# RMS norms of the differential heads in the grouped part, map combination split over two engines, grouped values in pairs

## The chip, the core and the metric

The kernel runs on one core of one Trainium2 chip. Its metric is the device time of one execution in microseconds (us), from launch to end, as the median of several runs. A core has five engines that each take their instructions in a fixed order and wait for one another by semaphores: TensorE (PE; its weight loads are shown apart as PEld), VectorE (DVE), ScalarE (ACT), GpSimd (POOL) and SyncE (SP, which issues the DMAs). Matmul results go to PSUM; the rest lies in SBUF.

## What is computed

A trunk of two layers over 1024 latent tokens with 256 context tokens in front, width 1024. The first layer's mixer is attention with two kinds of heads in parallel; the second layer's is a gated convolution; each layer has an MLP. The change lies in the first layer's attention, cut here to what matters:

```
def diff_attention(q, k, v, lam, lam_init, subln_g):      # 4 heads, each with two maps of width 64
    s = jnp.einsum('bqhid,bkhid->bhiqk', q, k) * (HEAD_DIM ** -0.5)
    p = jax.nn.softmax(s.astype(jnp.float32), axis=-1)
    attn = (p[:, :, 0] - lam * p[:, :, 1]).astype(v.dtype)
    o = jnp.einsum('bhqk,bkhe->bqhe', attn, v)
    o = rms_norm(o, subln_g) * (1.0 - lam_init)

def gqa_attention(q, k, v):                               # 8 query heads on 2 key/value heads
    s = jnp.einsum('bqgrd,bkgd->bgrqk', q, k) * (HEAD_DIM ** -0.5)
    p = jax.nn.softmax(s.astype(jnp.float32), axis=-1).astype(v.dtype)
    o = jnp.einsum('bgrqk,bkgd->bqgrd', p, v)
```

Queries are the 1024 latent tokens, keys all 1280 tokens.

## The kernel before

Attention is two stages, one after the other: the differential heads (some 291 to 516 us in the trace), then the grouped heads (to some 775 us). A scheduler orders each engine's instructions from the order in which the code emits them, with `high_priority` moving some forward; a tile's buffers are a ring of `bufs`, and an instruction that writes a tile waits until the buffer's last user is done.

**Differential stage.** `Attention.build` walks 32 steps: 4 heads, 4 units of 256 queries in each head, 2 steps of 128 queries in a unit. One step (`UnitA.scores`) makes two maps of 128 queries by 1280 keys. For each, `softmax` has TensorE write the scores `s` into three PSUM banks (L1135 and L1136; the ring of `s` holds two maps), VectorE find the row maxima `mx` (L1138), and ScalarE take the exponential `e` with its row sum `sm` (L1141). VectorE then combines the maps in one instruction over all 1280 keys, `e0 += cc * e1` (L1254), with `cc` from the two row sums (L1251, L1252). Two steps later TensorE transposes the combined map in ten pieces of 128 keys (L1150, in three groups of 4, 4 and 2 pieces, each into one PSUM tile `one`, of which there are two), ScalarE copies each group to `pt` (L1155), and per unit TensorE multiplies by the values (L1272), whose result ScalarE copies to `ot` (L1274). The maps aren't divided by their first row sum `s0`, so the RMS norm has a term with the square of `s0`: VectorE squares it (L1259), POOL multiplies the identity by it into `dg` (L1260). After every second unit `finish` does the norm of 512 queries: ACT squares `ot` (L1281), TensorE sums squares and adds the epsilon term (L1283, L1284), ACT copies the result (L1286) and makes a first inverse root in three instructions (L458 to L460), VectorE refines it (L461 to L463) and scales `ot` (L1289). There are eight such norms; six lie wholly between 300 and 510 us.

**Grouped stage.** `Grouped.build` walks 80 steps: eight blocks `j` (a pair of heads and 512 queries), ten key tiles `kt` in each. A step has the score matmuls of its key tile (L1381, L1382), two exponentials on ACT into `pt` (L1383), and the sum of the exponentials over key tiles into `e`, on POOL for `kt` 1 to 6 and on VectorE for 7 to 9 (L1387). For the next block, `maximum` runs ahead: three score matmuls (L1355) and three row maxima on VectorE (L1357) in each of the first eight steps; L1358 joins three maxima into `w`. Five PSUM banks (`bank`) are shared by exponentials and maxima: two and three of them in a step. Two steps later `values` multiplies by the values (L1396): two matmuls of 64 columns each, on the left and right half of TensorE's array. `divide` sums the row sums with ones (L1411, also on array halves), inverts them on ACT (L1414, L1415) and scales the block's result on VectorE (L1416 to L1418).

L1396 and L1411 are the only matmuls on array halves. In what follows a *stretch* is a row of such matmuls with no other matmul between them on TensorE.

Of the kernel before, what the change touches and what calls it, by code (L numbers as in the profile page):

```python
# [9 lines left out]
F32 = mybir.dt.float32  # L10
F32R = mybir.dt.float32r
AF = mybir.ActivationFunctionType
ALU = mybir.AluOpType
# [3 lines left out]
P = 128  # L17
# [7 lines left out]
KT = NC + NT  # L25
KEYS = KT * P
# [4 lines left out]
GROUPS = ((0, 4), (4, 4), (8, 2))  # L31
# [24 lines left out]
class Trunk:  # L56
# [34 lines left out]
    def build(self):  # L91
        nc = self.nc
        nc.scalar.preload_act_table_set("natural_log_exp_and_others")
        with self.pool("const") as cp:
            self.cp = cp
            self.constants()
            with self.pool("one", space=PSUM) as op, self.pool("dram", space=bass.MemoryType.DRAM) as dp:
                self.op, self.dp = op, dp
                self.main()
# [989 lines left out]
class Attention:  # L1089
# [36 lines left out]
                                           in1=q[s][r, :].bitcast(F32), op0=ALU.mult, op1=ALU.subtract)  # L1126
        return q

    def softmax(self, q, c, k):

        nc, pl = self.nc, self.pl
        s = self.pp.tile([P, 1536], F32, name="s", tag="s", bufs=2)
        for (g0, gn), (k1, k2) in zip(GROUPS, k):
            o = s[:, g0 * P:(g0 + gn) * P]
            nc.tensor.matmul(o, lhsT=q[:, c], rhs=k1[:, 0:gn * P], start=True, stop=False)  # L1135
            nc.tensor.matmul(o, lhsT=q[:, c], rhs=k2[:, 0:gn * P], start=False, stop=True)  # L1136
        mx = pl.tile([P, 1], F32, name="mx", bufs=4)
        nc.vector.reduce_max(out=mx, in_=s[:, 0:KEYS], axis=AX.X, negate=True)  # L1138
        e = pl.tile([P, KEYS], F32, name="e", tag="e", bufs=6)
        sm = pl.tile([P, 1], F32, name="sm", bufs=6)  # L1140
        nc.scalar.activation(e, s[:, 0:KEYS], AF.Exp, bias=mx, accum_out=sm)  # L1141
        return e, sm

    def transposed(self, e, pt, i):

        t, nc = self.t, self.nc
        for g, (g0, gn) in enumerate(GROUPS):
# [6 lines left out]
            o, v = pt[g][:, 0:gn, i * P:(i + 1) * P], tr[:, 0:gn * P].rearrange("p (k q) -> p k q", q=P)  # L1154
            nc.scalar.copy(out=o, in_=v)  # L1155

    def build(self):
        t = self.t
        units = self.units
        steps = [(u, i) for u in units for i in range(2)]  # L1160
        n = len(steps)
        psa = t.pool("ps2", space=PSUM)
        self.pp = psa.__enter__()

        def prepare(k):
            if k % 2 == 0 and 2 <= k + 2 < n:
                units[k // 2 + 1].prepare()
            elif k == n - 2:
                self.grouped = Grouped(self)
                self.grouped.prepare(0)  # L1170

        def weights(k):
            if 0 <= k - 2 < n:
                u, i = steps[k - 2]
                u.weights(i)

        def scores(k):
            if k < n:
                u, i = steps[k]
                u.scores(i)  # L1180

        def values(k):
            j = k - 2
            if 0 <= j < n and j % 2 == 1:
                units[j // 2].values()
                if j == n - 1:
                    t.first_weights()

        def finish(k):
            j = k - 4  # L1190
            if 0 <= j < n and j % 4 == 3:
                units[j // 2].finish()

        for k in range(n + 4):
            if k == n:
                psa.__exit__(None, None, None)
                psb = t.pool("ps3", space=PSUM)
                self.grouped.pp = psb.__enter__()
            for f, offset in ((prepare, 200), (weights, 100), (scores, None), (values, 0), (finish, 0)):
                if offset is None:  # L1200
                    f(k)
                else:
                    with t.tc.high_priority(offset=offset):
                        f(k)
            if k >= n:
                self.grouped.first(k - n)
        self.grouped.build()
        psb.__exit__(None, None, None)
# [27 lines left out]
class UnitA(Unit):  # L1236
# [8 lines left out]

    def scores(self, i):
        at, t, nc, pl, c = self.at, self.at.t, self.at.nc, self.at.pl, self.cols(i)
        e0, s0 = at.softmax(self.q[0], c, self.k[0])
        e1, s1 = at.softmax(self.q[1], c, self.k[1])
        cc = pl.tile([P, 1], F32, name="cc", bufs=4)  # L1250
        nc.vector.reciprocal(out=cc, in_=s1)  # L1251
        nc.vector.scalar_tensor_tensor(out=cc, in0=cc, scalar=s0, in1=t.nlam, op0=ALU.mult, op1=ALU.mult)  # L1252

        nc.vector.scalar_tensor_tensor(out=e0, in0=e1, scalar=cc, in1=e0, op0=ALU.mult, op1=ALU.add)  # L1254
        if self.b % 2 == 0 and i == 0:
            UnitA.state["dg"] = pl.tile([P, 512], F32, name="dg", tag="dg", bufs=2)
        self.dg = UnitA.state["dg"]
        c2 = pl.tile([P, 1], F32, name="c2", bufs=4)
        nc.vector.tensor_tensor(out=c2, in0=s0, in1=s0, op=ALU.mult)  # L1259
        nc.gpsimd.tensor_tensor(out=self.dg[:, c], in0=t.ident, in1=c2.broadcast_to([P, P]), op=ALU.mult)  # L1260
        self.e[i] = e0

    def weights(self, i):
# [4 lines left out]
    def values(self):  # L1268
# [3 lines left out]
            nc.tensor.matmul(pv[:, 0:256], lhsT=t.vA[kt][:, h * P:(h + 1) * P], rhs=self.pt[kt // 4][:, kt % 4, :],  # L1272
                             start=kt == 0, stop=kt == KT - 1)
        nc.scalar.copy(out=self.out(), in_=pv[:, 0:256])  # L1274

    def finish(self):

        at, t, nc, pl = self.at, self.at.t, self.at.nc, self.at.pl
        u = self.ot[:, (self.b - 1) * 256:(self.b + 1) * 256]
        sq = t.ut("sq")  # L1280
        nc.scalar.activation(sq, u, AF.Square)  # L1281
        nrm = at.one()
        nc.tensor.matmul(nrm, lhsT=t.sdiv, rhs=sq, start=True, stop=False)  # L1283
        nc.tensor.matmul(nrm, lhsT=t.sepsm, rhs=self.dg, start=False, stop=True)  # L1284
        v = t.ut("v2")
        nc.scalar.copy(out=v, in_=nrm)  # L1286
        y = t.ut("y")
        t.rsqrt0(y, sq, v)
        nc.vector.scalar_tensor_tensor(out=u, in0=u, scalar=t.subg, in1=y, op0=ALU.mult, op1=ALU.mult)  # L1289


class Grouped:

# [78 lines left out]
    def exponentials(self, j, kt):  # L1372
        nc, pl = self.nc, self.at.pl
        k1, k2 = self.k[j // 4][kt // 4]
        c = slice(kt % 4 * P, (kt % 4 + 1) * P)
        pt = self.pt[j, kt] = pl.tile([P, 2, 512], F32, name="pt", tag="pt", bufs=8)
        if kt == 0:
            self.sum[j] = pl.tile([P, KEYS], F32, name="e", tag="e", bufs=6)
        for s in range(2):
            o = self.bank()  # L1380
            nc.tensor.matmul(o, lhsT=k1[:, c], rhs=self.q[j][s], start=True, stop=False)  # L1381
            nc.tensor.matmul(o, lhsT=k2[:, c], rhs=self.q2[j][s], start=False, stop=True)  # L1382
            nc.scalar.activation(pt[:, s, :], o, AF.Exp)  # L1383
        f = self.sum[j][:, 0:1024].rearrange("p (s q) -> p s q", s=2)
        if kt > 0:
            eng = nc.gpsimd if kt < 7 else nc.vector
            eng.tensor_tensor(out=f, in0=self.pt[j, 0] if kt == 1 else f, in1=pt, op=ALU.add)  # L1387
# [40 lines left out]

    def build(self):
        n = 8 * KT  # L1430
        for k in range(n + 5):
            j, kt = divmod(k, KT)
            if k < n:
                if kt == 7 and j + 2 < 8:
                    self.prepare(j + 2)
                self.exponentials(j, kt)
                if j < 7:
                    self.ahead(j + 1, kt)
            if 0 <= k - 2 < n:
                j, kt = divmod(k - 2, KT)  # L1440
                self.values(j, kt)
                if kt == KT - 1:
                    self.finish(j)
            if k >= 5 and (k - 5) % KT == KT - 1:
                self.divide((k - 5) // KT)

    def ahead(self, j, m):
        with self.t.tc.high_priority(offset=40):
# [61 lines left out]
```

## Time and profile before

| | us |
|---|---|
| median of three runs | 2594.61 |
| their range | 2592.67 to 2594.73 |
| profiled execution, whole | 2599.33 |
| profiled execution, span from first to last instruction | 2597.6 |

The profiled execution lies 4.72 us above the median, and 1.7 us of it lie around the span. Over the span PE is busy for 94%, DVE for 75%, ACT for 48%, POOL for 15%. A matmul's busy time in the records includes its way through the array, so that successive matmuls overlap; the distance from one start to the next is the better measure of what a matmul takes from TensorE. The differential stage is about 225 us of the span, the grouped stage about 260 us.

### The profile page before, as it was taken

Reading aid. Unit: us, or ns where it says so; the run is one execution under the profiler, and the core shown is the slowest. Engines: PE = TensorE matmul, PEld = TensorE weight load, DVE = VectorE, ACT = ScalarE, POOL = GpSimd, SP = SyncE. Lnnn points to the kernel's source line nnn. Section 1 sums busy time; section 2 is a strip of 40 time slices with the busy share of each in tenths; the row PEclk is TensorE's granted clock in tenths of the full one; section 3 lists DMA queues with packets and bytes.
Section 4 is the critical chain, followed back from the end, with each engine's and each line's share of the span. In section 5 each row is a group of like instructions: output and inputs, shape, how many; then the busy total and the mean of one; then the engine's idle time right before and its main releaser. Section 6 shows DMA issues by size and latency. Waiting matters only on the chain. (4 is left out here: it accounts for less than half of the span.)

```text
span 2597.6 us, 29924 instructions
## 1 busy us (share of the span) xinstructions
PE 2433.4 (94%) x10706; PEld 1893.6 (73%) x10706; DVE 1946.2 (75%) x2980; ACT 1244.2 (48%) x2018; POOL 392.7 (15%) x245
## 2 busy tenths in 40 slices
PE   5999899999999879999899989999999999899997
PEld 3778677754547667787788777788777888688786
DVE  9877888887868877785756689766888555765867
ACT  3403477755552475454344346533348555334343
POOL 5101000034542410000000023100331000000002
PEclk7999899999999989999899999999999999899999
DMA  5551011000021047777642230123303445844231
GB/s 206 199 180 45 21 30 47 15 25 6 1 65 49 3 141 258 251 254 243 247 138 101 89 122 31 51 73 106 130 25 107 161 138 169 294 145 138 82 122 65
DMA packets 118517, 297.11 MB, mean 114 GB/s; under 512 B 13536, under 2 KB 19296, under 8 KB 118368
## 3 DMA queue, kind: packets, MB, share of 16 engines
q1 hardware_dynamic: 118368, 295.20, 33.8%
q8 instruction: 84, 1.38, 0.2%
q14 instruction: 65, 0.53, 0.1%
HBM read 225.29 MB, written 63.96 MB: 111 GB/s over the span
## 5 line engine op out<-in xcount | busy, mean ns | idle before, releaser
L74 PE MATMUL ps<-bl,part 128*128 128x512 f32 x784 | 308.9, 395 | 7.9 <-DVE bl L78 7.9
L73 PE MATMUL ps<-bh,part 128*128 128x512 f32 x784 | 309.3, 396 | 6.4 <-ACT part L909 6.4
L75 PE MATMUL ps<-bh,part 128*128 128x512 f32 x784 | 308.7, 397 | 5.8 <-DVE part L78 5.8
L909 ACT CAST part<-a 128x512 fp32r<-128x512 f32 x196 | 121.8, 623 | 305.0 <-PE ps L74 161.1
L78 DVE TENSOR_TENSOR part<-a,part 128x512 fp32r<-128x512 f32 x196 | 134.7, 689 | 160.7 <-ACT part L909 160.7
L73 PE MATMUL ps<-T,a 128*128 128x512 f32 x608 | 238.8, 393 | 9.7 <-DVE tmp L818 7.0
L74 PE MATMUL ps<-T,a 128*128 128x512 f32 x608 | 237.9, 391 | 2.2 <-DVE T L78 2.2
L75 PE MATMUL ps<-T,a 128*128 128x512 f32 x608 | 237.8, 391 | 0.0
L529 POOL TENSOR_TENSOR acc<-acc,mb 128x512 f32<-128x512 f32 x29 | 48.1, 1689 | 1074.2 <-ACT mb L526 1074.2
L78 DVE TENSOR_TENSOR a<-raw,a 128x1024 fp32r<-128x1024 f32 (+1 forms) x114 | 119.3, 1047 | 85.6 <-PE ps L74 75.0
L73 PE MATMUL ps<-H,a 128*128 128x512 f32 x456 | 178.8, 392 | 3.7 <-ACT a L533 3.7
L74 PEld LDWEIGHTS ps<-bl,part 128*128 128x128 f32 x784 | 150.0, 192 | 41.8 <-DVE bl L78 9.8
L75 PEld LDWEIGHTS ps<-bh,part 128*128 128x128 f32 x784 | 149.9, 191 | 38.8 <-DVE part L78 7.3
L74 PE MATMUL ps<-H,a 128*128 128x512 f32 x456 | 178.1, 391 | 0.0
L73 PEld LDWEIGHTS ps<-bh,part 128*128 128x128 f32 x784 | 149.4, 191 | 38.8 <-ACT part L909 7.6
L75 PE MATMUL ps<-H,a 128*128 128x512 f32 x456 | 177.7, 390 | 0.0
L818 DVE TENSOR_TENSOR tmp<-ps,tmp 128x512 f32<-128x512 f32 x114 | 78.5, 689 | 121.7 <-PE ps L75 84.2
L533 ACT CAST a<-raw 128x1024 fp32r<-128x1024 f32 (+1 forms) x114 | 100.9, 908 | 139.4 <-PE ps L74 95.7
L73 PEld LDWEIGHTS ps<-T,a 128*128 128x128 f32 x608 | 114.6, 188 | 38.0 <-DVE tmp L818 9.1
L74 PEld LDWEIGHTS ps<-T,a 128*128 128x128 f32 x608 | 114.7, 189 | 26.8 <-DVE T L78 3.5
L75 PEld LDWEIGHTS ps<-T,a 128*128 128x128 f32 x608 | 114.8, 189 | 24.0
L1357 DVE TENSOR_REDUCE mx<-s 128x1 f32<-128x512 f32 (+1 forms) x192 | 103.9, 593 | 36.6 <-PE s L1355 36.6
(414 smaller groups left out, 6020.0 us busy)
## 6 DMA issues: line engine op xcount, KB each, us to landing
gq<-tmp SPq DMA_DIRECT2D x196, 256.0 KB, 3.4
b<-gq SPq DMA_DIRECT2D x98, 512.0 KB, 3.3
raw<-in_w SPq DMA_DIRECT2D x72, 512.0 KB, 4.3
a<-in_w SPq DMA_DIRECT2D x140, 256.0 KB, 4.8
raw<-in_adaT SPq DMA_DIRECT2D x48, 512.0 KB, 4.9
adar<-in_adaT SPq DMA_DIRECT2D x32, 512.0 KB, 5.4
raw<-in_cw_in SPq DMA_DIRECT2D x24, 512.0 KB, 3.5
ada<-in_adaT SPq DMA_DIRECT2D x16, 512.0 KB, 6.8
```

Of the source, the lines that this page charges most:

```text
L73: mm(ps, lhsT=lh, rhs=rh, start=start, stop=False, **kw)
L74: mm(ps, lhsT=lh, rhs=rl, start=False, stop=False, **kw)
L75: mm(ps, lhsT=ll, rhs=rh, start=False, stop=stop, **kw)
L78: return eng.tensor_tensor(out=out, in0=a, in1=hi.bitcast(F32), op=ALU.subtract)
L529: self.eng(NORM[li, h]["sub"][j]).tensor_tensor(out=a, in0=a, in1=mb, op=ALU.subtract)
L533: self.nc.scalar.copy(out=hi, in_=src)
L818: nc.vector.tensor_tensor(out=o, in0=a, in1=b, op=op)
L909: self.tc.keep_in_program_order(nc.scalar.copy(out=hi, in_=src))
L1357: nc.vector.reduce_max(out=mx[:, g:g + 1], in_=o[:, 0:gn * P], axis=AX.X)
```

## The change

It has three parts. (1) `finish` becomes `Attention.norm`, and is called in the grouped stage, in steps 4, 9, 14, ... 39, one of the eight norms each time; the first row sums are kept in one tile `s0` of 32 columns, and POOL makes `dg` there with four one-input instructions per norm, in place of the DVE square and the POOL product of each map. (2) Of each combination VectorE does the first 512 keys; for the other 768, in pieces of 512 and 256, POOL first multiplies `e1` by `cc` and then adds it to `e0`, four instructions a step; the ring of `e` goes from 6 to 8 buffers. (3) `values` of the grouped stage is called for two key tiles at every second step, and `divide` one step later than before. The amounts of TensorE work stay the same.

```diff
-        nc.vector.scalar_tensor_tensor(out=e0, in0=e1, scalar=cc, in1=e0, op0=ALU.mult, op1=ALU.add)
-        nc.vector.tensor_tensor(out=c2, in0=s0, in1=s0, op=ALU.mult)
-        nc.gpsimd.tensor_tensor(out=self.dg[:, c], in0=t.ident, in1=c2.broadcast_to([P, P]), op=ALU.mult)
+        for g, (g0, gn) in enumerate(GROUPS):
+            a, b = [x[:, g0 * P:(g0 + gn) * P] for x in (e0, e1)]
+            if g == 0:
+                nc.vector.scalar_tensor_tensor(out=a, in0=b, scalar=cc, in1=a, op0=ALU.mult, op1=ALU.add)
+            else:
+                nc.gpsimd.tensor_scalar(out=b, in0=b, scalar1=cc, scalar2=1.0, op0=ALU.mult, op1=ALU.mult)
+                nc.gpsimd.tensor_tensor(out=a, in0=a, in1=b, op=ALU.add)
...
+    def norm(self, n):
+        t, nc = self.t, self.nc
+        u = t.oT[n // 2][:, n % 2 * 512:(n % 2 + 1) * 512]
+        dg, sq = t.ut("dg"), t.ut("sq")
+        for i in range(4):
+            s0 = self.s0[:, n * 4 + i:n * 4 + i + 1]
+            nc.gpsimd.tensor_scalar(out=dg[:, i * P:(i + 1) * P], in0=t.ident, scalar1=s0, scalar2=s0, op0=ALU.mult, op1=ALU.mult)
...
-            if 0 <= k - 2 < n:
+            if 0 < k - 2 < n and k % 2 == 1:
                 j, kt = divmod(k - 2, KT)
+                self.values(j, kt - 1)
                 self.values(j, kt)
...
-            if k >= 5 and (k - 5) % KT == KT - 1:
-                self.divide((k - 5) // KT)
+            if k >= 6 and (k - 6) % KT == KT - 1:
+                self.divide((k - 6) // KT)
+            if k % 5 == 4 and k < 40:
+                self.at.norm(k // 5)
```

The rest of `norm` is the text of `finish`, line for line. How the scheduler's order moves is shown at three places.

TensorE in the grouped stage, before, some steps into the second block (q and k are the queries and keys of the scores, s the PSUM banks, pv the values' sum):

```order
L1396 MATMUL pv<-pt,vB 64x512 x2
L1381 MATMUL s<-q_4868,k_4528 128x512
L1382 MATMUL s<-q_4870,k_4529 128x512
L1381 MATMUL s<-q_4869,k_4528 128x512
L1355 MATMUL s<-k_4528,q_5056 128x512
L1355 MATMUL s<-k_4539,q_5056 128x512
L1355 MATMUL s<-k_4550,q_5056 128x256
L1382 MATMUL s<-q_4871,k_4529 128x512
L1396 MATMUL pv<-pt,vB 64x512 x2
```

The same engine and block after, where a pair was not kept together:

```order
L1382 MATMUL s<-q_4949,k_4432 128x512
L1396 MATMUL pv<-pt,vB 64x512
L1381 MATMUL s<-q_4948,k_4431 128x512
L1355 MATMUL s<-k_4431,q_5231 128x512
L1355 MATMUL s<-k_4442,q_5231 128x512
L1355 MATMUL s<-k_4453,q_5231 128x256
L1382 MATMUL s<-q_4950,k_4432 128x512
L1396 MATMUL pv<-pt,vB 64x512 x3
L1381 MATMUL s<-q_4947,k_4442 128x512
```

A value matmul stands alone, and three follow later in one stretch. In the whole order of TensorE there are 92 stretches before (28 of one matmul, 56 of two, 7 of two with a `divide`, one of six with a `divide`) and 63 after (23 of one, 4 of two, 14 of three, 15 of four, 6 of three or four with one or both of a `divide`'s, one of eight with both).

VectorE in the grouped stage, before, in a block's middle (mx and w are maxima):

```order
L1357 TENSOR_REDUCE mx_5183<-s 128x1 x3
L1357 TENSOR_REDUCE mx_5207<-s 128x1
L1358 TENSOR_REDUCE w<-mx_5183 128x1
L1357 TENSOR_REDUCE mx_5207<-s 128x1 x2
L1358 TENSOR_REDUCE w<-mx_5207 128x1
```

After, around the third norm:

```order
L1357 TENSOR_REDUCE mx_5184<-s 128x1 x3
L1358 TENSOR_REDUCE w<-mx_5184 128x1
L461 TENSOR_TENSOR sq<-sq,v_5164 128x512
L462 TENSOR_SCALAR sq<-sq 128x512
L463 TENSOR_TENSOR y<-y,sq 128x512
L1173 SCALAR_TENSOR_TENSOR ot<-ot,subg,y 128x512
L1357 TENSOR_REDUCE mx_5219<-s 128x1 x3
```

The norm's four instructions stand between the maxima of two steps. The fifth norm stands in the same way; the others have maxima or other work between their four.

POOL in the differential stage had one `dg` product a step. After, its order in that stage is this, 32 times over:

```order
L1275 TENSOR_SCALAR e<-e,cc 128x512
L1275 TENSOR_SCALAR e<-e,cc 128x256
L1276 TENSOR_TENSOR e<-e 128x512
L1276 TENSOR_TENSOR e<-e 128x256
L1275 TENSOR_SCALAR e<-e,cc 128x512
```

The transposes of a map's second and third group wait for its third and fourth row. Behind the attention the order of every engine is the same as before.

## Rows read from the trace of the kernel before

**Rows 1.** Windows view: length, busy us (count) of PE, PEld, DVE, ACT, POOL; clock.

```profile
300.00:510.00 210.00, 198.03 (x1051) 155.32 (x1050) 184.04 (x250) 161.87 (x289) 17.02 (x35) 0.99 0.12 29
530.00:770.00 240.00, 236.57 (x915) 114.42 (x915) 181.03 (x308) 129.43 (x227) 117.87 (x51) 1.00 0.07 22
```

**Rows 2.** Groups by line, 300 to 510 us: busy us, mean ns, idle before.

```profile
L1254 DVE SCALAR_TENSOR_TENSOR e<-e,cc 128x1280 f32<-128x1280 f32 x30 | 46.5, 1550 | 0.8
...
L1283 PE MATMUL one<-sq,sdiv 128*128 128x512 f32 x12 | 6.1, 592 | 0.0
L1284 PE MATMUL one<-dg,sepsm 128*128 128x512 f32 x12 | 6.1, 591 | 0.0
...
L1289 DVE SCALAR_TENSOR_TENSOR ot<-ot,subg,y 128x512 f32<-128x512 f32 x6 | 4.5, 746 | 0.1
L463 DVE TENSOR_TENSOR y<-y,sq 128x512 f32<-128x512 f32 x6 | 4.2, 692 | 0.2
L461 DVE TENSOR_TENSOR sq<-sq,v 128x512 f32<-128x512 f32 x6 | 4.1, 688 | 4.8 <-ACT sq L460 4.8
...
L462 DVE TENSOR_SCALAR sq<-sq 128x512 f32<-128x512 f32 x6 | 2.6, 427 | 0.2
```

**Rows 3.** Waits view, 300 to 515 us: us in total, times, longest.

```profile
PEld s L1135 <- ACT e L1141: 14.5, 26, 2.0
ACT e L1141 <- DVE mx L1138: 13.1, 17, 1.6
PEld one L1150 <- ACT pt L1155: 12.5, 33, 1.5
...
PE one L1150 <- DVE e L1254: 0.9, 1, 0.9
```

**Rows 4.** Timeline of the differential stage: start, length, what; in brackets idle before.

```profile
390.73 1.55 DVE L1254 SCALAR_TENSOR_TENSOR e<-e,cc 128x1280 f32<-128x1280 f32 x1
...
393.13 1.47 DVE L1138 TENSOR_REDUCE mx<-s 128x1 f32<-128x1280 f32 x1
...
396.11 0.50 PE L1135 MATMUL s<-k,q 128*128 128x512 f32 x1 [0.72 <-ACT e L1141]
```

**Rows 5.** Timeline of PE in the grouped stage (a half matmul is two records).

```profile
592.99 1.07 PE L1396 MATMUL pv<-pt,vB 128*64 128x512 f32 x2
593.99 0.50 PE L1381 MATMUL s<-q,k 128*128 128x512 f32 x1
...
602.92 0.40 PE L1382 MATMUL s<-q,k 128*128 128x512 f32 x1
...
603.25 1.08 PE L1396 MATMUL pv<-pt,vB 128*64 128x512 f32 x4
...
604.26 0.50 PE L1381 MATMUL s<-q,k 128*128 128x512 f32 x1
...
604.59 0.39 PE L1382 MATMUL s<-q,k 128*128 128x512 f32 x1
...
604.82 0.40 PE L1381 MATMUL s<-q,k 128*128 128x512 f32 x1
...
608.67 1.08 PE L1396 MATMUL pv<-pt,vB 128*64 128x512 f32 x4
...
610.53 0.50 PE L1381 MATMUL s<-q,k 128*128 128x512 f32 x1
```

**Rows 6.** One line (ns min/median/max), then the timeline around its first instance.

```profile
L1417 DVE SCALAR_TENSOR_TENSOR r<-ra,r x8: 680/2698/2802, 586.8 to 774.6; 128x512 f32<-128x512 f32 x8
```

```profile
586.82 2.70 DVE L1417 SCALAR_TENSOR_TENSOR r<-ra,r 128x512 f32<-128x512 f32 x1
...
590.16 1.61 DVE L1357 TENSOR_REDUCE mx<-s 128x1 f32<-128x512 f32 x3
590.18 0.50 PE L1381 MATMUL s<-q,k 128*128 128x512 f32 x1
```

**Rows 7.** POOL's groups by line and form, whole span.

```profile
L1387 POOL TENSOR_TENSOR e<-e,pt 128x1024 f32<-128x1024 f32 x40 | 96.5, 2411 | 23.3 <-ACT pt L1383 22.7 <-DVE mx L1357 0.3
...
L78 POOL TENSOR_TENSOR wlo<-wraw,whi 128x512 fp32r<-128x512 f32 x8 | 10.2, 1296 | 157.3 <-ACT whi L230 157.3
...
L1306 POOL MEMSET w<- 128x512 f32 x2 | 1.0, 526 | 0.0
```

More of the change, by code (lines that the diff above doesn't have):

```diff
@@ L1127, in qstack, with softmax @@
         return q
-    def softmax(self, q, c, k):
+    def softmax(self, q, c, k, sm=None):
         nc, pl = self.nc, self.pl
@@ L1138, in softmax @@
         nc.vector.reduce_max(out=mx, in_=s[:, 0:KEYS], axis=AX.X, negate=True)
-        e = pl.tile([P, KEYS], F32, name="e", tag="e", bufs=6)
-        sm = pl.tile([P, 1], F32, name="sm", bufs=6)
+        e = pl.tile([P, KEYS], F32, name="e", tag="e", bufs=8)
+        sm = pl.tile([P, 1], F32, name="sm", bufs=6) if sm is None else sm
         nc.scalar.activation(e, s[:, 0:KEYS], AF.Exp, bias=mx, accum_out=sm)
@@ L1155, in transposed @@
             nc.scalar.copy(out=o, in_=v)
+    def norm(self, n):
[5 more added lines that the diff above has]
+            nc.gpsimd.tensor_scalar(out=dg[:, i * P:(i + 1) * P], in0=t.ident, scalar1=s0, scalar2=s0, op0=ALU.mult, op1=ALU.mult)
+        nc.scalar.activation(sq, u, AF.Square)
+        nrm = self.one()
+        nc.tensor.matmul(nrm, lhsT=t.sdiv, rhs=sq, start=True, stop=False)
+        nc.tensor.matmul(nrm, lhsT=t.sepsm, rhs=dg, start=False, stop=True)
+        v = t.ut("v2")
+        nc.scalar.copy(out=v, in_=nrm)
+        y = t.ut("y")
+        t.rsqrt0(y, sq, v)
+        nc.vector.scalar_tensor_tensor(out=u, in0=u, scalar=t.subg, in1=y, op0=ALU.mult, op1=ALU.mult)
     def build(self):
         t = self.t
+        self.s0 = self.pl.tile([P, 32], F32, name="s0")
         units = self.units
@@ L1187, in values @@
                     t.first_weights()
[L1189 to L1192, printed above, removed]
         for k in range(n + 4):
@@ L1198, in build @@
                 self.grouped.pp = psb.__enter__()
-            for f, offset in ((prepare, 200), (weights, 100), (scores, None), (values, 0), (finish, 0)):
+            for f, offset in ((prepare, 200), (weights, 100), (scores, None), (values, 0)):
                 if offset is None:
@@ L1247, in scores @@
         at, t, nc, pl, c = self.at, self.at.t, self.at.nc, self.at.pl, self.cols(i)
-        e0, s0 = at.softmax(self.q[0], c, self.k[0])
+        n = (self.h * 4 + self.b) * 2 + i
+        s0 = at.s0[:, n:n + 1]
+        e0, _ = at.softmax(self.q[0], c, self.k[0], s0)
         e1, s1 = at.softmax(self.q[1], c, self.k[1])
@@ L1252, in scores @@
         nc.vector.scalar_tensor_tensor(out=cc, in0=cc, scalar=s0, in1=t.nlam, op0=ALU.mult, op1=ALU.mult)
-        nc.vector.scalar_tensor_tensor(out=e0, in0=e1, scalar=cc, in1=e0, op0=ALU.mult, op1=ALU.add)
[L1255 to L1258, printed above, removed]
-        nc.vector.tensor_tensor(out=c2, in0=s0, in1=s0, op=ALU.mult)
-        nc.gpsimd.tensor_tensor(out=self.dg[:, c], in0=t.ident, in1=c2.broadcast_to([P, P]), op=ALU.mult)
+        for g, (g0, gn) in enumerate(GROUPS):
[5 more added lines that the diff above has]
+                nc.gpsimd.tensor_tensor(out=a, in0=a, in1=b, op=ALU.add)
         self.e[i] = e0
@@ L1274, in values @@
         nc.scalar.copy(out=self.out(), in_=pv[:, 0:256])
[L1276 to L1289, printed above, removed]
 class Grouped:
@@ L1377, in exponentials @@
         if kt == 0:
-            self.sum[j] = pl.tile([P, KEYS], F32, name="e", tag="e", bufs=6)
+            self.sum[j] = pl.tile([P, KEYS], F32, name="e", tag="e", bufs=8)
         for s in range(2):
@@ L1430, in build @@
         n = 8 * KT
-        for k in range(n + 5):
+        for k in range(n + 6):
             j, kt = divmod(k, KT)
```

## The prediction

> **What bounds the kernel now.** I read the windows view first, for one stretch of each stage. Between 300 and 510 us PE is busy for 198.0 of 210 us and DVE for 184.0, 88% [rows 1]; ACT and POOL are well below. So TensorE leads, but it idles for 12.0 us, and DVE is close behind it. Between 530 and 770 us PE is busy for 236.6 of 240 us and DVE for 181.0 [rows 1]: here TensorE alone is the bound, and whatever adds to its work or makes it wait shows in the time.
>
> The waits view says what holds TensorE in the first stage. Its weight loads wait for exponentials (14.5 us, scores that need a PSUM buffer back) and for copies (12.5 us), together 27.0 us, while ACT waits 13.1 us for row maxima [rows 3]. The timeline shows one link: the combination starts on DVE at 390.73 and takes 1.55 us, the next maximum starts only at 393.13, and at 396.11 the next scores start after 0.72 us of idle PE that the exponential ended [rows 4]. DVE's lateness passes through ACT to TensorE. The combination itself hardly delays a transpose: one wait of 0.9 us [rows 3].
>
> **DVE's relief in the differential stage.** Of 1.550 us per step [rows 2] 768/1280 goes, 0.93 us, 29.8 us over 32 steps. The refinement and scaling of a norm is 0.688 + 0.427 + 0.692 + 0.746 = 2.55 us [rows 2]; six leave the stretch of rows 1, 15.3 us. DVE's 184.0 us there falls by 30 x 0.93 + 15.3 = 43 to 141 us, and it is no longer a near bound. What TensorE gains is bounded below by nothing (ACT's own chain may be late instead) and above by the 27.0 us that its loads wait. I take 12, PE's idle time, close also to the 13.1 us for which ACT waits for DVE: **-12 us** (0 to -27).
>
> **POOL's share of the combination.** No one-input multiplication on POOL stands in the trace. A fill of 512 columns takes 0.526 us and a two-input subtraction of 512 columns 1.296 us [rows 7]; the true value should lie by the fill, since the multiplication streams one tensor. With half for 256 columns the four instructions take 0.53 + 0.26 + 1.30 + 0.65 = 2.7 us, or 3.9 us if the multiplication costs as much as the subtraction. From `cc` on, the last keys are ready 2.7 to 3.9 us later in place of 1.55, so 1.2 to 2.3 us later than now, and a DVE combination of 0.62 us that stands in POOL's way may come on top. POOL has room: 32 x 2.7 to 3.9 us is 87 to 125 us in a stage of over 200. But TensorE's transposes of the second and third group now wait for POOL, and behind a late transpose stand ACT's copy and, on ACT's queue, the next exponential. Bounds: nothing (the transposes come two steps later) and a wait at every step, 32 x 1.2 = 38 us. In the new order the transposes of some steps in each head follow the scores by little more than one pair of maps; I put 12 of 32 steps at 0.4 us: **+5 us**.
>
> **The norms' TensorE work** only changes its place. Its busy time is 2 x 0.59 x 2 = 2.4 us a norm [rows 2], less from start to start. Six or seven norms, 12 to 14 us at most, leave one stage and arrive in the other, where nothing hides them. If the first stage is led by TensorE, as rows 1 say, the sum is **0**; if DVE or ACT led it, up to +14 us would be lost. The norm's ACT work (five instructions) goes to a stage where ACT is busy for 129.4 of 240 us [rows 1], and costs nothing there.
>
> **Pairs of value tiles.** A stretch of two half matmuls takes 604.26 - 603.25 = 1.01 us until the next score matmul; one with a `divide` behind it takes 610.53 - 608.67 = 1.86, so 0.85 us for the addition. A lone half takes 593.99 - 592.99 = 1.00 us, the same as two, since the halves run beside each other [rows 5]. Around a stretch the neighbours are drawn apart too: 0.33 us into it (602.92 to 603.25) and 0.33 between the first two score matmuls behind it, against 0.23 between the next ones [rows 5]. So each stretch has a fixed cost of (1.01 - 0.85) + 0.10 + 0.10 = 0.36 us, and each unit of one or two halves 0.85 us. The order has 92 stretches before and 63 after: -29 x 0.36 = -10.4 us. But the scheduler breaks many pairs open, and I count 102 units before and 107 after (a stretch of three is two units): +5 x 0.85 = +4.3 us. Together **-6 us**; between -10.4 (if broken pairs cost nothing) and -3.
>
> **DVE in the grouped stage.** It takes up seven more norms, 7 x 2.55 = 18 us, on 181 of 240 [rows 1], so 80 to 85%. That alone is no bound. But DVE instructions with two SBUF inputs stand still there while POOL runs its sums: L1417 takes 0.680 us at least and 2.698 in the median, a wait of 2.0 us [rows 6], about a POOL sum of 2.41 us [rows 7]. The Trainium skill ("SBUF — State Buffer", section "SBUF: two separate sides") says that DVE and GpSimd share one pair of SBUF ports under an exclusive lock, held for a whole instruction, for DVE instructions with two SBUF inputs or in a 2-port mode; L1417's two levels agree with it. By that rule nearly every moved norm instruction waits, which is the second rival. Here: one such wait is absorbed. DVE's 3.3 us from 586.82 push the next maxima to 590.16, and PE goes on at 590.18 in its usual spacing [rows 6], since the five PSUM banks hold one more step. Where the four instructions stand in a row, as in the third and fifth norm of the new order, I reckon 2.55 us and two to three waits, 6.5 to 8.5 us, less the 3.3 that are absorbed and what DVE regains: 3 us each. The other six cost up to 0.3 us. **+7 us**, between 0 and 8 x (2.55 + 4 x 2.0 - 3.3) = 58, the upper end only if every norm stands in a row and always meets a sum; 20 is as far as I take it into the range.
>
> **The sum**, against the profiled execution: -12 + 5 + 0 - 6 + 7 = -6 us, 2599.33 to 2593.3. That execution is 4.72 us above the median of the runs, so the median goes from 2594.61 to **2588.6 us**. The larger ring of `e` and the `divide` one step later cost nothing: the stage's last instructions keep their order.
>
> **Rivals.** *POOL is too slow for the transposes.* It decides if the multiplication costs like the subtraction: then a map is ready 2.3 us later than now, and with 24 steps that wait 0.9 us (the size of the one wait today [rows 3]) the term is +22 in place of +5: -6 + 17 = +11, 2605 us. Against it: two steps lie between a map and its use.
>
> *DVE is locked out in the grouped stage.* If five norms instead of two meet POOL's sums with three waits and more, at 4 to 5 us of idle TensorE each, the term is +22 in place of +7: +9, 2604 us, slower than before. It decides once DVE's maxima come more than one step late. For it: POOL is busy for 117.9 of 240 us [rows 1], nearly all of it within `kt` 1 to 6. Against it: maxima stand between most of the norms' instructions.
>
> *TensorE runs nearly free.* If the lag of maxima was all that held it, the first term is -22 instead of -12, and DVE absorbs its norms (+3 in place of +7): -6 - 10 - 4 = -20, 2575 us.
>
> That the change does not do what it says is so in part already: pairs are broken, and it stands in the sum.
>
> **How the numbers follow.** The forecast has 0.50, around 2588.6 with 2582 to 2595; TensorE free 0.15; POOL late 0.14; DVE locked out 0.21. A measurement of this kernel can tell 0.2%, 5.2 us, from no change: 2589.4 to 2599.8. Faster: 0.30 of the forecast's 0.50, and 0.15: 0.45. Same: the other 0.20, and 0.08 of the rivals whose price comes out smaller: 0.28. Slower: the remaining 0.27. From 2576 to 2604 no more than 2 in 10 is left out: half of the 0.15 below, a third of the 0.35 above.
>
> **What would show it.** Right: in the differential stage ACT waits for `mx` for a few us instead of 13.1, PE's idle time falls, L1254's successor takes about 0.62 us, and the stage is some 17 to 20 us shorter; the grouped stage is 5 to 15 us longer, with fewer L1396 stretches and norm instructions on DVE of up to 2.7 us. Wrong: transposes that wait for POOL by more than 10 us in total (the first rival), score matmuls that wait for DVE's maxima in the grouped stage by more than 10 us (the second), POOL multiplications of over 1 us, or lone halves that cost less than 1.00 us.

## The result and the profile after

The changed kernel takes 2609.77 us (median of 11 runs, 2605.54 to 2613.74) where the kernel before takes 2594.73 in the same comparison: a ratio of 1.0054, with a 95% interval of 1.0043 to 1.0064. By the ratio it is slower by 14 us; the prediction was 6 us faster. The profiled execution took 2611.26 us, with a span of 2609.5.

I read the stages first. The differential stage runs from the first score matmul (L1135) to the first matmul of the grouped maxima (L1355), the grouped stage from there to the last value matmul (L1396); what lies after it is alike to 2.4 us and has the same order of instructions.

| profiled execution | before | after | difference |
|---|---|---|---|
| ahead of the first score | 291.3 | 289.8 | -1.5 |
| differential stage | 224.4 | 219.7 | -4.7 |
| grouped stage | 255.4 | 271.0 | +15.6 |
| behind it | 1826.5 | 1828.9 | +2.4 |

The prediction had the first stage 17 to 20 us shorter and the second 5 to 15 us longer. The second came out just beyond that; the first missed by 13 us.

The windows view of the changed kernel answers [rows 1] (length, then busy us and count of PE, PEld, DVE, ACT, POOL; clock):

```profile
300.00:510.00 210.00, 192.26 (x1050) 151.37 (x1049) 150.59 (x198) 150.87 (x266) 115.04 (x129) 0.99 0.12 29
530.00:770.00 240.00, 230.15 (x873) 114.00 (x873) 183.71 (x316) 133.48 (x244) 127.54 (x77) 1.00 0.02 4
```

DVE is busy for 33 us less in the first stretch (the working said 43). But PE idles *more* than before: 17.7 of 210 us in place of 12.0. In the second stretch it idles 9.9 of 240 in place of 3.4. The granted clock is the same in all these stretches.

What PE itself waited for between 300 and 510 us (waits view: us in total, times, longest), first before, then after:

```profile
PE s L1135 <- ACT e L1141: 7.3, 14, 1.8
PE one L1150 <- ACT pt L1155: 2.0, 2, 1.3
```

```profile
PE one L1150 <- ACT pt L1155: 6.7, 10, 1.6
PE s L1135 <- ACT e L1141: 3.2, 4, 1.7
PE one L1150 <- POOL e L1276: 2.1, 4, 0.7
PE one L1150 <- DVE e L1273: 2.0, 1, 2.0
```

Two things are seen here. Before, scores waited for exponentials for 7.3 us on PE itself. The 14.5 us of [rows 3] belong to the weight loads, which wait while earlier matmuls still run, so about half of them cost nothing. And after, that wait did fall, by 4.1 us; but transposes now wait 4.7 us longer for ScalarE's copies, and 2.1 us for POOL.

POOL's share, in groups by line and form between 300 and 510 us (busy us, mean ns; L1273 is VectorE's part, L1275 the multiplication, L1276 the addition):

```profile
L1276 POOL TENSOR_TENSOR e<-e 128x512 f32<-128x512 f32 x31 | 40.4, 1302 | 0.0
...
L1275 POOL TENSOR_SCALAR e<-e,cc 128x512 f32<-128x512 f32 x31 | 35.5, 1146 | 146.6 <-DVE cc L1267 57.5 <-DVE cc L1268 50.1 <-ACT q L1124 22.9
...
L1273 DVE SCALAR_TENSOR_TENSOR e<-e,cc 128x512 f32<-128x512 f32 x31 | 25.5, 822 | 2.0
L1276 POOL TENSOR_TENSOR e<-e 128x256 f32<-128x256 f32 x31 | 24.8, 801 | 0.0
...
L1275 POOL TENSOR_SCALAR e<-e,cc 128x256 f32<-128x256 f32 x31 | 14.7, 475 | 0.0
```

One step's chain on POOL is 1.15 + 0.48 + 1.30 + 0.80 = 3.7 us, where the prediction took 2.7, with 3.9 as its upper end. VectorE's part takes 0.82 us, not 0.62.

### The profile page after: what moved, and what is told of

Its sections match the earlier page's. It is cut to its first block, busy times and chain, and to the rows that moved or that the text cites. A ratio compares the mean times of both kernels' runs of the same rounds, so it can differ in the third digit from the quotient of the medians.

```text
span 2609.5 us, 30137 instructions
## 1 busy us (share of the span) xinstructions
PE 2436.1 (93%) x10706; PEld 1898.6 (73%) x10706; DVE 1918.1 (74%) x2948; ACT 1239.7 (48%) x2018; POOL 512.1 (20%) x373
## 5 line engine op out<-in xcount | busy, mean ns | idle before, releaser
L74 PE MATMUL ps<-hid,w 128*128 128x512 f32 (+1 forms) x336 | 127.5, 380 | 5.3 <-POOL hid L78 5.3
```

Source lines behind the costliest of these rows:

```text
L74: mm(ps, lhsT=lh, rhs=rl, start=False, stop=False, **kw)
```

## The experiments

Each was timed in at least five rounds beside the kernel before. The stages are those of each run's profiled execution, cut as above; "alone" means on the kernel before. A single stage scatters less than a whole time, since the stretch ahead of the first score varies by some 5 us from one run to another, and the one behind the stages by as much. The differential stage of the five kernels that leave it alone (before, e1, e6, e11, e12) takes 224.4 to 225.8 us, so that differences of 1 to 2 us in it are no more than that scatter; each stage time stands on one execution.

| run | ratio to before, 95% interval | differential | grouped |
|---|---|---|---|
| before | 1 | 224.4 | 255.4 |
| after | 1.0054 [1.0043, 1.0064] | 219.7 | 271.0 |
| e1 pairs alone | 0.9996 [0.9987, 1.0004] | 225.3 | 254.2 |
| e2 norms alone | 1.0051 [1.0039, 1.0063] | 215.9 | 282.6 |
| e3 split alone | 1.0035 [1.0023, 1.0047] | 233.6 | 255.2 |
| e4 relief without POOL | 0.9987 [0.9978, 0.9996] | 223.2 | 255.0 |
| e5 after, no split | 1.0041 [1.0027, 1.0055] | 213.6 | 282.1 |
| e6 right half first, pairs | 0.9944 [0.9932, 0.9957] | 224.7 | 241.1 |
| e7 relief, late transposes | 1.0051 [1.0038, 1.0063] | 236.0 | 260.0 |
| e8 late transposes | 1.0052 [1.0040, 1.0065] | 236.8 | 255.3 |
| e9 after, short sums | 1.0007 [0.9998, 1.0016] | 219.8 | 260.9 |
| e10 shorter maximum | 1.0003 [0.9994, 1.0012] | 220.3 | 260.9 |
| e11 as e6, earlier divide | 0.9953 [0.9939, 0.9966] | 225.1 | 242.9 |
| e12 groups of 2, 4, 4 | 0.9918 [0.9905, 0.9932] | 225.8 | 235.4 |
| e13 after, short share | 1.0044 [1.0031, 1.0058] | 215.8 | 272.7 |

### Each part alone (e1, e2, e3)

Theory 1 was that VectorE had never held TensorE in the differential stage; its rival, theory 2, that the relief was real and POOL's lateness ate it. e1 takes the third part of the change alone (`values` twice at every second step, `divide` one step later), e2 the first (`finish` becomes `norm`), e3 the second (the loop over `GROUPS` in place of L1254, and 8 buffers of `e`); their edits are those pieces of the change's diff.

> The kernel before with part (3) alone: values of two key tiles at every second step, divide one step later; the order has 65 stretches in place of 92, and 111 units in place of 102. By the price of the prediction (0.36 us a stretch, 0.85 a unit): -27 x 0.36 + 9 x 0.85 = -2.1 us. If a broken pair costs nothing, -10 us. If the grouped stage also loses time because value matmuls that come later hold `pt` buffers, up to +3.

Measured: -1 us, within what can be told from no change; the grouped stage is 1.2 us shorter. That rules out the -10 of whole pairs. It agrees with the price of stretches and units with its broken pairs (-2.1), and as well with nothing.

> The kernel before with part (1) alone: all eight norms in the grouped stage, the combination whole on VectorE, values as before. Theory 1 (TensorE was not held by VectorE in the differential stage; the norms' matmuls leave it, 10 to 12 us, and arrive in the grouped stage, where waits for row maxima of 6 to 9 us come on top): +5 to +11 us, with the differential stage 8 to 12 us shorter. Theory 2 (VectorE's relief is worth its price to TensorE): the differential stage 16 us or more shorter, the whole -3 to +3.

Measured: +13 us. The differential stage loses 8.5 us, the grouped stage gains 27.2. That is theory 1, and worse than it: TensorE's work of the moved norms leaves the first stage at no more than its own length, though VectorE got 15 us of relief with it.

> The kernel before with part (2) alone: the last 768 keys of each combination on GpSimd, ring of `e` of 8, norms in the differential stage. Theory 1 (VectorE's relief gives TensorE nothing, and the transposes wait for GpSimd): +3 to +8 us. Theory 2 (relief of some 12 us, GpSimd's lateness takes most of it back): -4 to 0. As in the prediction (relief 12, lateness 5): -7.

Measured: +9 us, all in the differential stage (+9.2). POOL's share alone costs more than any theory said.

### VectorE's relief by itself (e4), and another order (e7, e8)

```diff
-        nc.vector.scalar_tensor_tensor(out=e0, in0=e1, scalar=cc, in1=e0, op0=ALU.mult, op1=ALU.add)
+        nc.vector.scalar_tensor_tensor(out=e0[:, 0:512], in0=e1[:, 0:512], scalar=cc, in1=e0[:, 0:512], op0=ALU.mult, op1=ALU.add)
```

> The kernel before, but of each combination VectorE does only the first 512 keys and nothing does the other 768, which stay uncombined: that part of the computation is left out, so that the time shows what VectorE's relief is worth when no other engine takes the work. Theory 1: within 3 us of before. Theory 2: -10 to -14 us, most of it in the waits of scores for exponentials.

Measured: -3.4 us (interval 1 to 6), of which 1.2 in the differential stage. So 26 us taken from VectorE are worth a microsecond or two to TensorE in that stage: theory 1. The instructions stand in the same order on TensorE, ScalarE and VectorE in e3 and e4, so that the 10.4 us between their stages (233.6 and 223.2) are put down to POOL's share alone; the larger ring of `e` in e3 is the only other difference. PE's waits of e4 between 300 and 510 us show how the relief was lost:

```profile
PE one L1150 <- ACT pt L1155: 7.7, 11, 1.6
PE s L1135 <- ACT e L1141: 1.7, 2, 1.1
```

Beside the rows of before above: scores wait 5.6 us less for exponentials, transposes 5.7 us more for ScalarE's copies. The scheduler knows how long VectorE's instructions take, and with shorter ones it sets another order: rows of exactly ten transposes without a matmul between them, none in the order before, are eleven in e4 and five in the changed kernel. A row of ten needs three of the two PSUM tiles `one`, and so waits for copies.

Theory 3 was that these rows are the loss. e7 and e8 take the transposes' priority away, on e4 and on the kernel before:

```diff
-            for f, offset in ((prepare, 200), (weights, 100), (scores, None), (values, 0), (finish, 0)):
+            for f, offset in ((prepare, 200), (weights, 0), (scores, None), (values, 0), (finish, 0)):
```

> As the run of VectorE's relief alone (keys 512 to 1279 of each combination left out), but with the transposes at the priority of the code around them in place of 100 ahead: the ten transposes of a map no longer stand in one row (1 row of 10 or more in place of 12). Theory 3 (the relief is given back because the scheduler then sets ten transposes in a row, which wait for ScalarE's copies of the two PSUM tiles): 6 to 12 us faster than the relief alone. If the row costs nothing, within 3 us of it, so -2 to -6 us against before.

> The kernel before with the transposes at the priority of the code around them in place of 100 ahead, nothing else. Its rows of eight and more transposes go from 12 to 9. Theory 3: -2 to -6 us. If the order of the transposes is worth nothing: within 2 us. If what matters is that transposes come early, because ScalarE's copies then come early: +3 or more.

Measured: both slower by 13 us; the differential stage is 12 to 13 us longer than in the same kernel with the priority. In this form theory 3 falls. Rows of ten or more go from 12 in e4 to 5 in e7 (the expectation had 1), and PE's waits for copies with them (7.7 to 0.2 us); but its scores wait for exponentials again (1.7 to 10.6 us), and late transposes cost as much in e8, whose order had no row of exactly ten to break. What the pair does show is the relief's worth in a second order: 236.0 with it, 236.8 without. Even that 0.8 is no gain, as some 1.7 us of value and norm matmuls stand in e7's grouped stage (260.0) that stand in e8's differential one.

### A shorter way from scores to exponentials (e10)

```diff
-        nc.vector.reduce_max(out=mx, in_=s[:, 0:KEYS], axis=AX.X, negate=True)
+        nc.vector.reduce_max(out=mx, in_=s[:, 0:512], axis=AX.X, negate=True)
```

> The kernel before, but the row maximum in the differential stage is taken over the first 512 of 1280 keys (the rest of the maximum is left out; any shift gives the same softmax here). VectorE gets some 0.9 us a map, 56 us in all, and each map's exponential can start 0.9 us earlier after its scores. Theory 4 (TensorE waits for the time from scores to maximum to exponential, with two score buffers, not for a busy VectorE): the differential stage is 8 to 14 us shorter. If only TensorE's own work and order count, it is within 3 us, as with 30 us of relief by a shorter combination (-1.2).

Measured: no difference; the differential stage is 4.1 us shorter, the grouped one 5.5 us longer. About 2 us of those 4.1 are values, transposes and a norm matmul that this order has behind the first maximum of the grouped stage. Twice the relief, and exponentials that can start earlier, thus give half or less of what theory 4 asked for. So neither VectorE's time nor the way from scores to exponentials is what the stage is long by.

### The split inside the changed kernel (e5, e13)

e5 is the changed kernel with L1254 of before in place of the split and six buffers of `e`. In e13 the split stays, with POOL's instructions cut short:

```diff
-                nc.gpsimd.tensor_scalar(out=b, in0=b, scalar1=cc, scalar2=1.0, op0=ALU.mult, op1=ALU.mult)
-                nc.gpsimd.tensor_tensor(out=a, in0=a, in1=b, op=ALU.add)
+                nc.gpsimd.tensor_scalar(out=b[:, 0:32], in0=b[:, 0:32], scalar1=cc, scalar2=1.0, op0=ALU.mult, op1=ALU.mult)
+                nc.gpsimd.tensor_tensor(out=a[:, 0:32], in0=a[:, 0:32], in1=b[:, 0:32], op=ALU.add)
```

> The changed kernel without part (2): norms in the grouped stage, values in pairs, the combination whole on VectorE and the ring of `e` of 6. If GpSimd's share costs in the changed kernel what it cost alone (+9), this is +5 us against before. If it costs only the +4 by which the changed kernel's differential stage (219.7 us) is longer than that of the norms alone (215.9), +10. If VectorE's relief was worth 12 us after all, and was only hidden, +20.

> The changed kernel, but each of GpSimd's four instructions of a combination works on 32 columns in place of 512 and 256 (the other columns of the last 768 keys stay uncombined: that part is left out). The order on every engine is that of the changed kernel. If GpSimd's lateness made the 6 us between the differential stage of the changed kernel (219.7) and of that with the combination whole on VectorE (213.6), the stage is 211 to 214 us and the whole 6 to 9 us faster than the changed kernel. If VectorE's relief is worth the 12 us of the prediction and GpSimd's lateness hid it, 202 to 206. If the other order made them, 218 to 220 and the whole as the changed kernel.

Measured: e5 +10.7, e13 +11.5 us. That agrees with the +10 that e5 expected if the share costs only 4 us here. The differential stages say more than the times, whose intervals overlap: 213.6 without the split, 215.8 with the split's order and relief but little lateness of POOL, 219.7 with all of it. The 215.8 lie between the 211 to 214 of POOL's lateness alone and the 218 to 220 of the order alone. What shorter instructions of POOL win is 3.9 us here, less than the 10.4 of e3 against e4. The relief of VectorE, with the order that comes with it, is not a gain but +2.2.

### VectorE and POOL in the grouped stage (e9)

```diff
-            eng.tensor_tensor(out=f, in0=self.pt[j, 0] if kt == 1 else f, in1=pt, op=ALU.add)
+            a = self.pt[j, 0] if kt == 1 else f
+            r = slice(0, 64) if 1 < kt < 7 else slice(0, 512)
+            if kt == 7:
+                nc.vector.scalar_tensor_tensor(out=f, in0=f, scalar=1.0, in1=pt, op0=ALU.add, op1=ALU.add)
...
+                eng.tensor_tensor(out=f[:, :, r], in0=a[:, :, r], in1=pt[:, :, r], op=ALU.add)
```

> The changed kernel, but of GpSimd's sums of exponentials for `kt` 2 to 6 only the first 64 of 512 queries of each head are added (the rest is left out; at `kt` 7 VectorE adds 1.0, so that no sum is near zero). On every engine the instructions stand in the same order as in the changed kernel; GpSimd's sums only get short. Theory 5 (the waits of 9 us that the grouped stage gained are VectorE instructions that stand still while GpSimd sums): the norm's four instructions on VectorE take 0.43 to 0.75 us each, the two waits of 2.7 us at the third and the fifth norm shrink below 1 us, the stage is 6 to 12 us shorter than 271.0. Rival (the four instructions themselves, 2.55 us in a row, make the maxima late): the two waits stay above 1.5 us, the stage within 3 us of 271.

Measured: +2 against before, so 12 us faster than the changed kernel; the grouped stage is 260.9 in place of 271.0, the differential one the same. Theory 5 holds, with 10.1 us, though the two waits shrink to 0.73 us and not to nothing. The timeline of the changed kernel around its third norm (start, length, what; in brackets idle before):

```profile
561.50 2.46 POOL L1387 TENSOR_TENSOR e<-pt 128x1024 f32<-128x1024 f32 x1 [6.61 <-ACT pt L1383]
...
561.96 2.54 DVE L461 TENSOR_TENSOR sq<-sq,v 128x512 f32<-128x512 f32 x1 [0.68 <-ACT sq L460]
...
564.44 2.34 POOL L1387 TENSOR_TENSOR e<-e,pt 128x1024 f32<-128x1024 f32 x1 [0.49 <-ACT pt L1383]
564.53 2.54 DVE L462 TENSOR_SCALAR sq<-sq 128x512 f32<-128x512 f32 x1
566.99 1.61 DVE L1357 TENSOR_REDUCE mx<-s 128x1 f32<-128x512 f32 x3
...
567.73 0.50 PE L1381 MATMUL s<-q,k 128*128 128x512 f32 x1 [2.62 <-DVE mx L1357]
```

The same place in e9 (its L1392 is the sum):

```profile
560.06 2.53 DVE L461 TENSOR_TENSOR sq<-sq,v 128x512 f32<-128x512 f32 x1 [0.67 <-ACT sq L460]
...
562.55 0.46 POOL L1392 TENSOR_TENSOR e<-e,pt 128x128 f32<-128x128 f32 x1 [0.52 <-ACT pt L1383]
562.62 0.68 DVE L462 TENSOR_SCALAR sq<-sq 128x512 f32<-128x512 f32 x1
563.22 1.60 DVE L1357 TENSOR_REDUCE mx<-s 128x1 f32<-128x512 f32 x3
...
563.95 0.50 PE L1381 MATMUL s<-q,k 128*128 128x512 f32 x1 [0.73 <-DVE mx L1357]
```

Both kernels have one norm instruction that meets a full sum (`kt` 1, 2.5 us). In the changed kernel the next meets the next sum, for another 2.5 us, and the maxima behind it come too late for PE by 2.62 us; in e9 by 0.73. One sum is nearly absorbed, two in a row are not. Over the stage PE's waits for these maxima (waits view, changed kernel, then e9) go from 6.6 us to 1.5:

```profile
PE s L1381 <- DVE mx L1357: 6.6, 4, 2.6
PE s L1355 <- DVE mx L1357: 2.3, 3, 0.8
```

```profile
PE s L1381 <- DVE mx L1357: 1.5, 2, 0.7
```

### A version that beats both (e6, e11, e12)

Pairs of halves break because the left half's exponential is done first, and the scheduler sends its matmul ahead at once. With the right half's matmul first in the code, the one that has to wait leads:

```diff
-        for s in range(2):
+        for s in (1, 0):
             nc.tensor.matmul(self.pv[j][s * 64:(s + 1) * 64, :], lhsT=t.vB[:, kt, g * 64:(g + 1) * 64], rhs=pt[:, s, :],
```

> The kernel before with values in pairs of key tiles (divide as before), and the right half's matmul ahead of the left one's in the code: the half whose exponential comes last is then the first in the queue, and few pairs of halves are broken: 59 stretches and 90 units, before 92 and 102. By the price of the prediction: -33 x 0.36 - 12 x 0.85 = -22 us, all of it in the grouped stage. If only stretches have a price, -12. If lone halves and switches cost nothing on TensorE's path, 0.

> As the run with the right half ahead and values in pairs, with divide one step earlier than before, where it stands beside a pair of value matmuls: 52 stretches in place of 59, 90 units as there. By the price of 0.36 us a stretch -2.5 us against that run, so -16 to -17 against before; nothing, so -14, if the sums of a block's last key tiles are not ready for it.

> The right half ahead as there, and values in groups of 2, 4 and 4 key tiles of a block: 49 stretches and 88 units. By the price -5 us against the run with pairs of 59 stretches and 90 units: -19 against before. Rival: with eight `pt` buffers, four key tiles that wait for their values hold up the exponentials, and TensorE waits for ScalarE: -5 to -12 against before.

e6 adds to this the pairs of the change with `divide` as before, e11 calls `divide` one step earlier, e12 calls `values` for key tiles 0 and 1, 2 to 5 and 6 to 9 of a block together. Stretches of one lone half go from 28 before to 4 in e6. Measured: -14.5, -12 and -21 us. The whole gain lies in the grouped stage (-14.3, -12.5, -20.0). By the price of stretches and units it would have been -22, -25 and -27 against before: half to three quarters of it arrive. e11 is not told apart from e6, so its seven stretches less were not seen to be worth anything. In e12's grouped stage a stretch of three whole pairs (12 records) reads

```profile
640.89 2.80 PE L1396 MATMUL pv<-pt,vB 128*64 128x512 f32 x12
643.62 0.66 PE L1364 MATMUL one<-ident,w 128*128 128x128 f32 x4
```

that is 2.73 us: three times 0.85 and a fixed 0.18, where the prediction had 0.85 and 0.16 from [rows 5]. The rival of e12, too few `pt` buffers, does not show.

## Why the prediction was wrong, step by step

The two stages add up to +10.9 us in the profiled executions. The runs divide them so; the pairs get what the other lines leave, so that the lines must add up:

| step | predicted | shown | from |
|---|---|---|---|
| VectorE's relief, with the order it brings | -12 | +2.2 | e5 to e13, differential stage |
| POOL's share | +5 | +3.9 | e13 to after |
| norms' TensorE work | 0 | -10.8 and about +10.3 | before to e5; 13 matmuls of 0.86 us, less 0.8 us of transposes and values that come earlier |
| pairs | -6 | about -5 | what is left of the grouped stage's +15.6 |
| VectorE locked out | +7 | +10.1 | e9 to after |

**VectorE's relief is the step that failed**, and it alone turns the sum's sign. Three things were wrong in it. It took PE's whole idle time of [rows 1], 12.0 us, as due to VectorE, since it lay near the 13.1 us for which ACT waits for maxima; PE's own waits for exponentials were 7.3. It sized the relief in proportion to the columns (0.93 us a step); an instruction of 512 takes 0.75 where nothing is in its way, so 0.80 are saved. Above all it kept TensorE's order as given. The relief did shorten the wait it was aimed at, in e4 by 5.6 us, and the transposes gave 5.7 back. The sign to watch, ACT's waits for `mx`, went the other way too, from the 13.1 us of [rows 3] to 21.2 (waits view of after, 300 to 510 us):

```profile
DVE mx L1138 <- PE s L1136: 42.5, 24, 7.9
...
ACT e L1141 <- DVE mx L1138: 21.2, 23, 1.9
```

That wait is no measure of VectorE's load: VectorE itself now waits 42.5 us for scores.

What the stage is long by instead is shown in part: a relief of 26 us (e4, 1.2 us; e7 against e8, 0.8 us) or 51 us (e10, 64 maxima of 0.69 us in place of 1.48; 4.1 us) hardly moves it. That the return comes from the new order is read from the waits and the rows of ten transposes; it wasn't shown by a run, as the order can't be held while VectorE's durations change. That stays open.

**POOL's share** was sized right by two errors that cancel. Its chain is 3.7 us, not 2.7: about half of that difference is what the prediction said "may come on top" and didn't add, the time in which VectorE's part stands in POOL's way. And some transposes follow their map much closer than the two steps that stood against the first rival: in the first timeline of the last section the second group of transposes starts when POOL's first addition on the same map has just ended. But most of the waits are short. With the norms left where they were, the same share costs 10.4 us (e3 against e4); the first rival had 22. The signs given for it are met in half: multiplications over 1 us, but only 2.1 us of PE's waits put down to POOL's additions.

**The norms' TensorE work** came as predicted: what leaves (8.5 us in e2, 10.8 in e5) arrives. Before, 13 of the 16 norm matmuls stand in the differential stage. Each takes 0.86 us from start to start (timeline of e9, grouped stage):

```profile
568.66 1.02 PE L1167 MATMUL one<-sq,sdiv 128*128 128x512 f32 x2
569.52 1.02 PE L1168 MATMUL one<-dg,sepsm 128*128 128x512 f32 x2
```

TensorE leads both stages, so moving its work between them is worth nothing.

**Pairs**: with 63 stretches and 107 units the price said -6, and about -5 is left for them. That is the least certain line: e2 and e5 differ by the pairs alone, and by 0.5 us in that stage, though there the clock (below) may hide some 5 us. e6 and e12 bear the price out in direction and order, not in full; e1 (-1.2 for a price of -2.1) is too small to tell.

**VectorE locked out**: the mechanism was right to the place. The third and the fifth norm, whose four instructions stand in a row, each stop PE by 2.6 us. The size, 10.1, is nearer to the 7 of the sum than to the 22 of the second rival; its sign, over 10 us of score matmuls' waits for maxima, was nearly met with 6.6 + 2.3. The 10.1 are an upper end for the norms: e9 shortens the sums for every VectorE instruction, and PE's waits for maxima fall by 7.4 of them.

In e2 and e5, with the same norms, the grouped stage is 11 us longer still. In e5 that is mostly the clock. During PE's waits or within 2 us of their end the granted clock falls to 0.50, the lower of its two levels (1.2 GHz), four times and for 20.4 us in all. One such stretch in the windows view, and the six value matmuls in it, first in e5, then in the changed kernel:

```profile
563.70:570.50 6.80, 6.32 (x12) 2.74 (x13) 4.28 (x10) 0.60 (x1) 2.86 (x1) 0.50 0.00 0
```

```profile
566.40 3.68 PE L1390 MATMUL pv<-pt,vB 128*64 128x512 f32 x6
```

```profile
568.97 1.93 PE L1396 MATMUL pv<-pt,vB 128*64 128x512 f32 x6
```

The changed kernel has the same two waits of 2.6 us and a clock of 1.00 all through that stage. e13, with the changed kernel's order, has 3.4 us at 0.50 there and is 1.7 us longer (272.7 against 271.0). At half a microsecond for each one at 0.50, an estimate from these rows, the clock makes 10 of e5's 11.1 us and 5 of e2's 11.6, which has 10.2 us at 0.50. Why the same waits lower it in one execution and not in another isn't shown. The rest of e2's, some 6 us, would fit the pairs that it lacks, which stays open.

The range ended at 2604; its upper end held the rivals one at a time, and no rival said that the first term was simply absent. With 0 in its place the sum is +6 and the time 2601.

## What to carry to other kernels

Waits of weight loads and of engines off the path overlap with work; what an edit can win is bounded by the idle time of the leading engine that ends at that wait, here 7.3 us and not 12 or 27. Where a scheduler sets the order, a shorter instruction on one engine is also another order on the others: count how the leading engine's rows change before crediting the relief. And where two engines share work that one release starts, look in the trace whether an instruction gets longer beside the other engine's: POOL's multiplication took 1.15 us here where it takes 0.69 by itself.

## What the runs showed of the hardware

POOL's multiplication of 512 columns takes 0.69 us at the least, yet its mean in the changed kernel is 1.15. The timeline shows why:

```profile
424.01 0.75 DVE L1273 SCALAR_TENSOR_TENSOR e<-e,cc 128x512 f32<-128x512 f32 x1
...
424.11 1.67 POOL L1275 TENSOR_SCALAR e<-e,cc 128x512 f32<-128x512 f32 x2 [3.47 <-DVE cc L1268]
...
425.75 1.96 POOL L1276 TENSOR_TENSOR e<-e 128x512 f32<-128x512 f32 x2
...
427.08 0.66 PE L1150 MATMUL one<-ident,e 128*128 128x128 f32 x4 [0.49 <-POOL e L1276]
...
428.11 0.75 DVE L1273 SCALAR_TENSOR_TENSOR e<-e,cc 128x512 f32<-128x512 f32 x1
...
428.27 1.15 POOL L1275 TENSOR_SCALAR e<-e,cc 128x512 f32<-128x512 f32 x1 [0.56 <-DVE cc L1268]
```

The same `cc` releases both engines, VectorE starts first, and POOL's first instruction stands still until VectorE's two-input one is done: the row of 428.27 ends 0.56 us after VectorE's. It waits and isn't merely slower, as e13 shows: on 32 columns the same instruction takes 0.29 us in five steps and 0.75 to 0.85 us in 26, about the same half microsecond on top as with 512. The prediction had named this possibility and given it no price. The Trainium skill ("SBUF — State Buffer", section "SBUF: two separate sides") has it that whichever starts first holds the shared pair for the whole instruction; these rows (VectorE first) and those of the third norm above (POOL first) agree.

A one-input instruction is held up as well: L462 takes 0.43 us before [rows 2] and 2.54 us beside a sum. The maxima, which read PSUM, are not: three take 1.60 us with a sum beside them, here in the changed kernel, and 1.61 without one at 566.99 us.

```profile
569.18 1.60 DVE L1357 TENSOR_REDUCE mx<-s 128x1 f32<-128x512 f32 x3
569.81 2.38 POOL L1387 TENSOR_TENSOR e<-e,pt 128x1024 f32<-128x1024 f32 x1 [3.02 <-ACT pt L1383]
```
